# Out projection of a hybrid encoder layer: the residual rows of x read by plain loads and added by VectorE in place of accumulating DMAs

## The chip, the core and the metric

One core of a Trainium2 chip runs the whole layer as a single program. The metric is the device time of one execution in microseconds (us); the number compared is the median over runs. TensorE (PE) does the matmuls, ScalarE (ACT) and VectorE (DVE) empty its PSUM banks and do the elementwise work, GpSimd (POOL) does small scalar chains and issues the accumulating DMAs, and SyncE (SP) issues all other DMAs from one queue, in order.

## The reference, cut to what matters

The input `x` has 2048 rows (tokens) of 1024 floats. The layer mixes tokens, projects the mixed rows `y` with `w_out`, normalises the result and adds the input rows:

```python
y = jnp.concatenate([ya, yh.astype(ya.dtype)], axis=-1) @ w_out[l]
h = h + rms_norm(y, g_mix_post[l])          # h is x here
u = rms_norm(h, g_x_pre[l])
m = rms_norm(mem, g_mem[l])
y = cross_attention(u, m, wq_x[l], wk_x[l], wv_x[l], wo_x[l])
h = h + rms_norm(y, g_x_post[l])
```

The change concerns the second of these lines alone: `x` is added to the normalised projection. A SwiGLU feed-forward follows, with a residual of its own.

## The kernel before

The kernel works in fp32 and makes each product of two matrices from three products of rounded halves. The second half of the program is a list of **jobs** (`jobs`): the out projection, the cross-attention scores, the values, the feed-forward. A job is a list of blocks. A block of the out projection is 256 tokens (two row tiles of 128 tokens, `n` and `n + 1`) by all 1024 columns; the job has eight. By a Strassen scheme a block takes seven products instead of eight, so seven **steps**, each of 4 x 3 = 12 matmuls of 512 columns. The first two blocks and the last two run as pairs, their steps alternating; the four between run one by one.

`phases` walks through the steps. After the matmuls of a step it does the following, in this order: it notes the newest ACT and DVE instructions (`mark`), advances each open **after-generator** by one `yield`, splits a weight operand that has been loaded, and starts at most one load of half a weight operand for a coming step (`half`). The after-generator of a block is opened at the block's last step, so its work runs in the steps of the blocks behind it. `behind` ties the ACT and DVE instructions of its block to follow those that `mark` noted.

For the out projection, `mixed_block` gives a block its functions. `out` empties a PSUM bank into a row tile `y[i]` (lines 1377 and 1379) and takes its mean square on ACT (line 1355). `after`, the subject of the change, does in its successive steps: (1) the two inverse roots on POOL (1366 to 1370), the scaling of row tile 0 on DVE (1403), the accumulating DMA that adds 128 rows of x into it (`add`, line 1384, issued by POOL), and its store to `h1_d` (line 78, SP); (2) the same for row tile 1; (3) nothing; (4) and (5) the mean squares of the two sums on ACT; (6) their inverse roots on POOL; (7) and (8) the transposition of each row tile on PE (line 1270), copied back over the row tile by ACT (1271) and stored to `h1t_d`, from where the scores read it. `h1_d` and `h1t_d` are DRAM buffers; the profile cuts their names, so that a store into `h1_d` reads `h_d<-row`.

Row tiles, 128 x 1024 floats or 512 KB, come from a pool of nine (`row_tile`). The pool serves `y` of the blocks, every half operand that `half` loads for the next job (`row<-qk_d`, `row<-qk_s`), and one operand of `combined`, which prepares sums of weights beside the blocks (its add is line 929). The program's order on each engine is chosen at build time by a scheduler that gives a tile its buffer once an earlier holder has let it go; the instruction that first writes the tile then waits for that holder. On SP all that stands behind such a wait, or behind a store that waits for its data, waits too.

Of the kernel before, what the change touches and what calls it, by code (L numbers as in the profile page):

```python
# [15 lines left out]
ALU = mybir.AluOpType  # L16
# [32 lines left out]
class Layer:  # L49
# [1336 lines left out]
    def mixed_block(self, n):  # L1386
        nc = self.nc
        y, ss = {}, []

        def out(i, j, a, b):  # L1390
            if not y:
                ss.append(self.small("q_s", 4))
                if not n:
                    self.g_mix_post = self.gain(self.I["g_mix_post"])
            if i not in y:
                y[i] = self.row_tile()
            self.squared(y[i][:, j * 512:(j + 1) * 512], a, b, ss[0][:, 2 * i + j:2 * i + j + 1])

        def after():
            r = self.rstds(ss[0])  # L1400
            s2 = self.small("q_s", 4)
            for i in range(2):
                nc.vector.scalar_tensor_tensor(y[i], y[i], r[:, i:i + 1], self.g_mix_post, ALU.mult, ALU.mult)
                self.add(y[i], self.I["x"], n + i)
                self.store(self.h1_d[(n + i) * P:(n + i + 1) * P, :], y[i])
                yield
            yield
            for i in range(2):
                self.mean_squares(y[i], i, s2)
                yield  # L1410
            r = self.rstds(s2)
            nc.gpsimd.tensor_scalar(self.r_x[:, n:n + 2], r, 1.0, None, ALU.mult)
            yield
            for i in range(2):
                self.store(self.h1t_d[n + i], self.transposed(y[i], y[i]))
                yield

        return self.tokens(self.y_d, n), out, after, None

    def score_block(self, n):  # L1420
# [231 lines left out]
```

## Time and profile before

| | |
|---|---|
| time, median of 3 runs | 2605.68 us (2604.11 to 2606.04) |
| the profiled execution | 2605.43 us |
| its span in the profile | 2603.6 us |
| PE busy | 2526.8 us, 97% of the span |
| DVE, ACT, POOL busy | 1744.2, 1262.3, 473.4 us |
| DMA moved | 497.88 MB, mean 191 GB/s |
| matmuls of the out projection | about 802 to 985 us of the span |
| their accumulating DMAs of x | 16, issued from 846.9 to 992.1 us |

The profile is one execution, in us from the start of its span. "Busy" of PE counts time in which any matmul runs. A line such as `PE pss L1270 <- DMA row<-in_x_dram: 4.6, 2, 2.5` says that PE, before instructions of line 1270 that write a `pss` bank, stood idle for 4.6 us in all, twice, at most 2.5 us, until a DMA from x into a row tile had landed. In the view of windows each row has a stretch, its length, the busy us of each engine with the number of instructions in brackets, the granted clock of PE as a share of full speed, the mean busy share of the 16 DMA engines, and what they moved. Queue q0 carries the DMAs that POOL issues, q1 those of SP. In the chain of waits a row has the start, the length, and what took that time.

### The profile page before, as it was taken

How to read it: one execution, taken by the hardware profiler on the slowest of the kernel's cores; microseconds unless marked ns; L12 is line 12 of the kernel's file. 1: busy time of each engine (PE TensorE's matmuls, PEld its weight loads, DVE VectorE, ACT ScalarE, POOL GpSimd, SP SyncE). 2: the span in 40 equal slices, each digit the busy share in tenths (PEclk: the TensorE clock that was granted, in tenths of full speed). 3: DMA queues.
4: the chain of work that ended last, by engine and by line, in shares of the span. 5: the costliest groups of instructions: out<-in, count | busy, mean ns of one | idle time of the engine just before them, and what ended most of it. 6: DMA issues, size and time to landing. Idle time of an engine off the chain costs nothing.

```text
span 2603.6 us, 34511 instructions
## 1 busy us (share of the span) xinstructions
PE 2526.8 (97%) x12160; PEld 2112.8 (81%) x12160; DVE 1744.2 (67%) x2773; ACT 1262.3 (48%) x2641; POOL 473.4 (18%) x651
## 2 busy tenths in 40 slices
PE   7989999999998999999989999999999999999998
PEld 6878788878897777888878888888888888888786
DVE  7675578887555568786885655576666656664756
ACT  5463366655554556565573333354333335443443
POOL 4240343320321324223320000000000000000022
PEclk9999999999999999999999999999999999999999
DMA  5434655484876998756994532353556434576798
GB/s 186 142 121 166 208 157 173 131 265 158 265 253 219 281 318 265 228 193 173 306 282 145 164 128 73 105 187 114 168 181 230 148 107 168 175 225 176 229 226 210
DMA packets 286350, 497.88 MB, mean 191 GB/s; under 512 B 20576, under 2 KB 143456, under 8 KB 286176
## 3 DMA queue, kind: packets, MB, share of 16 engines
q1 hardware_dynamic: 275520, 456.87, 52.4%
q0 software_dynamic: 10656, 38.80, 8.0%
q8 instruction: 96, 1.57, 0.2%
q14 instruction: 78, 0.64, 0.1%
HBM read 328.87 MB, written 166.72 MB: 190 GB/s over the span
## 4 chain that ended last, share of the span: by engine, by line
PE 80%; DMA 8%; DVE 4%; issue 3%; POOL 2%; ACT 2%; SPq 0%; DVEq 0%; POOLq 0%; ACTq 0%
PE psm L1018 22%; PE psm L1020 22%; PE psm L1019 22%; PE psg L161 2%; PE psg L163 2%; PE psg L162 2%; DMA row<-in_x_dram 1%; PE pss L1270 1%; DMA row<-h_d 1%; ACT junk L1355 1%; DMA x<-in_w_out_dram 1%; DVE S L885 1%; DMA h_d<-row 1%; DMA pair<-in_x_dram 1%; DMA kk<-z_d 1%
## 5 line engine op out<-in xcount | busy, mean ns | idle before, releaser
L1018 PE MATMUL psm<-T,S 128*128 128x512 f32 x2664 | 1034.9, 392 | 24.6 <-ACT S L882 13.5
L1019 PE MATMUL psm<-T,S 128*128 128x512 f32 x2664 | 1041.1, 391 | 0.0
L1020 PE MATMUL psm<-T,S 128*128 128x512 f32 x2664 | 1036.1, 391 | 3.8 <-DVE S L885 3.8
L1018 PEld LDWEIGHTS psm<-T,S 128*128 128x128 f32 x2664 | 502.2, 189 | 132.7 <-ACT S L882 15.3
L1020 PEld LDWEIGHTS psm<-T,S 128*128 128x128 f32 x2664 | 501.9, 188 | 111.0 <-DVE S L885 6.9
L1019 PEld LDWEIGHTS psm<-T,S 128*128 128x128 f32 x2664 | 502.3, 189 | 103.0
L882 ACT ACTIVATE S<-sum 128x512 fp32r<-128x512 f32 (+1 forms) x338 | 208.1, 619 | 341.4 <-PE psm L1020 333.1
L885 DVE TENSOR_TENSOR S<-sraw,S 128x512 fp32r<-128x512 f32 (+1 forms) x311 | 214.2, 696 | 223.4 <-ACT S L882 213.4
L885 DVE TENSOR_TENSOR S<-sum,S 128x512 fp32r<-128x512 f32 (+1 forms) x404 | 276.8, 689 | 81.6 <-ACT S L882 63.7
L1033 ACT ACTIVATE part<-psm 128x512 f32<-128x512 f32 x297 | 175.1, 592 | 178.0 <-PE psm L1020 172.8
L882 ACT ACTIVATE S<-sraw 128x512 fp32r<-128x512 f32 (+1 forms) x272 | 166.8, 617 | 156.0 <-PE psm L1020 143.0
L1384 POOL DMA_DIRECT2D row<-y_d x28 | 25.0, 892 | 1132.5 <-DMA sraw<-hid_d 964.5
L1355 ACT ACTIVATE junk<-row 128x512 f32<-128x512 f32 x160 | 99.7, 625 | 118.2 <-DVE row L1377 34.9
L885 DVE TENSOR_TENSOR T<-row,T 128x1024 fp32r<-128x1024 f32 x104 | 123.1, 1191 | 30.5 <-ACT T L882 30.2
L161 PE MATMUL psg<-u,whi 128*128 128x512 f32 x352 | 141.1, 401 | 1.6 <-POOL whi L145 1.6
L163 PE MATMUL psg<-u,wlo 128*128 128x512 f32 x352 | 139.5, 396 | 0.9 <-DVE wlo L146 0.9
L162 PE MATMUL psg<-u,whi 128*128 128x512 f32 x352 | 139.6, 396 | 0.0
L882 ACT ACTIVATE T<-row 128x1024 fp32r<-128x1024 f32 x104 | 105.7, 1027 | 20.7 <-DMA row<-in_w_down_dram 10.3
L884 POOL TENSOR_SCALAR S<-sum 128x512 fp32r<-128x512 f32 x66 | 50.5, 765 | 238.7 <-PE psm L1020 148.3
L1536 DVE TENSOR_TENSOR part<-psm,part 128x512 f32<-128x512 f32 x66 | 45.4, 688 | 65.3 <-PE psm L1020 65.2
L146 DVE TENSOR_TENSOR wlo<-raw,whi 128x1024 fp32r<-128x1024 f32 x54 | 68.7, 1271 | 29.1 <-ACT whi L143 22.4
L1527 DVE TENSOR_TENSOR row<-psm,part 128x512 f32<-128x512 f32 x66 | 45.4, 689 | 57.6 <-PE psm L1020 57.5
(329 smaller groups left out, 3651.3 us busy)
## 6 DMA issues: line engine op xcount, KB each, us to landing
sraw<-in_w_gate_dram SPq DMA_DIRECT2D x44, 512.0 KB, 4.9
sraw<-in_w_up_dram SPq DMA_DIRECT2D x44, 512.0 KB, 4.8
hid_d<-row SPq DMA_DIRECT2D x44, 512.0 KB, 2.7
h_d<-row SPq DMA_DIRECT2D x32, 512.0 KB, 6.9
y_d<-row SPq DMA_DIRECT2D x32, 512.0 KB, 3.8
sraw<-hid_d SPq DMA_DIRECT2D x32, 512.0 KB, 5.2
row<-h_d POOLq DMA_DIRECT2D x30, 512.0 KB, 7.5
row<-y_d POOLq DMA_DIRECT2D x28, 512.0 KB, 7.3
```

What stands on the lines that cost most here:

```text
L146: nc.vector.tensor_tensor(lo, raw, f32(hi), ALU.subtract)
L161: nc.tensor.matmul(ps, ah, bh, start=(i == 0), stop=False)
L162: nc.tensor.matmul(ps, ah, bl, start=False, stop=False)
L163: nc.tensor.matmul(ps, al, bh, start=False, stop=(i == n - 1))
L882: self.nc.scalar.activation(hi, raw, AF.Copy)
L884: self.nc.gpsimd.tensor_scalar(hi, raw, 1.0, 1.0, ALU.mult, ALU.mult)
L885: self.nc.vector.tensor_tensor(lo, raw, f32(hi), ALU.subtract)
L1018: nc.tensor.matmul(ps, s[:, 0, k, :], t[:, 0, k, :], start=st, stop=False, **kw)
L1019: nc.tensor.matmul(ps, s[:, 0, k, :], t[:, 1, k, :], start=False, stop=False, **kw)
L1020: nc.tensor.matmul(ps, s[:, 1, k, :], t[:, 0, k, :], start=False, stop=sp, **kw)
L1033: nc.scalar.activation(t, ps, AF.Copy)
L1355: self.nc.scalar.activation(junk, a, AF.Square, scale=float(D) ** -0.5, accum_out=to)
```

## The change

In `after` of the out projection's blocks, two row tiles are taken at the first step and filled by plain loads of x from SP's queue (`rows_of`). The accumulating DMAs are gone; in their place DVE adds the loaded rows, in steps of their own. The sequence becomes: (1) two loads, the roots, the scaling of row tile 0; (2) the scaling of row tile 1; (3) add and store of row tile 0; (4) add and store of row tile 1; (5) and (6) the mean squares; (7) the roots; (8) and (9) the transpositions. The empty step is gone, and what follows it comes one step later.

```diff
         def after():
+            x = [self.rows_of(self.I["x"], n + i) for i in range(2)]
             r = self.rstds(ss[0])
             s2 = self.small("q_s", 4)
             for i in range(2):
                 nc.vector.scalar_tensor_tensor(y[i], y[i], r[:, i:i + 1], self.g_mix_post, ALU.mult, ALU.mult)
-                self.add(y[i], self.I["x"], n + i)
+                yield
+            for i in range(2):
+                with self.behind():
+                    nc.vector.tensor_tensor(y[i], y[i], x[i], ALU.add)
                 self.store(self.h1_d[(n + i) * P:(n + i + 1) * P, :], y[i])
                 yield
-            yield
             for i in range(2):
                 self.mean_squares(y[i], i, s2)
                 yield
```

## The prediction

> **What bounds the kernel now.** I read the page first, then the view of windows around the 16 accumulating DMAs.
>
> ```profile
> PE 2526.8 (97%) x12160; PEld 2112.8 (81%) x12160; DVE 1744.2 (67%) x2773; ACT 1262.3 (48%) x2641; POOL 473.4 (18%) x651
> ```
>
> ```profile
> 846.00:860.00 14.00, 14.00 (x68) 11.65 (x67) 10.58 (x13) 5.79 (x14) 6.76 (x7) 1.00 0.82 182
> 860.00:945.00 85.00, 77.21 (x365) 63.19 (x364) 46.68 (x61) 45.85 (x113) 27.32 (x49) 0.98 0.95 302
> 945.00:985.00 40.00, 39.91 (x184) 32.56 (x183) 32.81 (x40) 28.29 (x55) 10.79 (x16) 1.00 1.03 353
> 985.00:1020.00 35.00, 31.66 (x154) 25.72 (x153) 27.90 (x36) 21.77 (x51) 18.50 (x23) 1.00 0.92 270
> 1020.00:1180.00 160.00, 160.00 (x771) 133.35 (x770) 130.22 (x238) 94.83 (x221) 39.16 (x53) 1.00 0.61 204
> ```
>
> PE bounds the program: 97% busy. What a change outside PE can win is PE's idle time. From 846 to 1020 us that is 174 - (14.00 + 77.21 + 39.91 + 31.66) = 11.2 us, and the DMA engines are 82% to 103% busy there. From 1020 to 1180, with the DMA engines at 61%, PE never idles. So the stage with the adds is the one disturbed, and the transfers are what is tight in it. Next, who kept PE waiting in that stretch:
>
> ```profile
> PE pss L1270 <- DMA row<-in_x_dram: 4.6, 2, 2.5
> PE psm L1018 <- DVE row L1377: 2.7, 1, 2.7
> PE pss L1270 <- ACT row L1271: 2.5, 2, 2.1
> PE psm L1020 <- DVE S L885: 1.3, 1, 1.3
> ```
>
> These make 11.1 us, all of the idle time. The chain of waits tells what stood behind each:
>
> ```profile
> 878.23 8.85 DMA row<-in_x_dram
> 887.09 6.46 DMA h_d<-row
> ...
> 899.77 12.85 DMA extra<-qk_d
> ...
> 923.85 10.20 DMA row<-in_x_dram
> 934.18 1.83 PE pss L1270 x8
> 936.01 0.43 PE psm L1018
> ...
> 938.24 0.23 PE psm L1018
> ...
> 995.10 9.72 DMA g<-vo_d
> ```
>
> Two stalls (4.6 us) are PE itself waiting for an accumulating DMA before it can transpose the row tile. The second has a tail: PE comes back at half speed, 0.43 us a matmul against 0.23, for five matmuls (1.0 us), and eight transpositions take 1.83 us where 0.88 is the full-speed length in the same chain:
>
> ```profile
> 967.01 0.88 PE pss L1270 x8
> ```
>
> That is 0.95 more, so a tail of about 1.9 us. The 2.5 us behind ACT are a step further on: ACT copies the transposed tile back over the row tile, must wait until the store of h1 has read it, and that store waits for the accumulating DMA. The 2.7 us hang on a weight load that took 12.85 us in the crowded DMA engines while DVE, in order, stood at line 929; the 1.3 us on another such load (9.72 us). Two more views show how far the accumulating DMA holds others, first ACT's waits, then SP's:
>
> ```profile
> ACT junk L1355 <- DMA row<-in_x_dram: 29.2, 8, 8.1
> ```
>
> ```profile
> SPq L78 <- DMA row<-in_x_dram: 54.3, 13, 9.5
> ```
>
> **The change part by part.** *Removed: 16 accumulating DMAs.* The view of DMA from 820 to 1010 us gives the price of a transfer of either kind.
>
> ```profile
> q1 hardware_dynamic: 16337, 43.18, 62.9%
> q0 software_dynamic: 2304, 8.39, 23.5%
> ...
> row<-in_x_dram POOLq DMA_DIRECT2D x16, 512.0 KB, 9.7
> h_d<-row SPq DMA_DIRECT2D x16, 512.0 KB, 7.3
> row<-qk_d SPq DMA_DIRECT2D x14, 512.0 KB, 6.8
> ...
> extra<-qk_d SPq DMA_DIRECT2D x3, 512.0 KB, 8.6
> ```
>
> q0 is the 16 adds: 23.5% of 190 us is 44.7 us of all engines, 2.79 us each. q1 moved 43.18 MB in 62.9%, 119.5 us, so 1.45 us for each 0.524 MB. A plain load in place of an add saves 1.34 us, 21 us for 16: the load on the engines over these 190 us falls from 86% to 75%. POOL loses 16 issues, which cost it a cheap row:
>
> ```profile
> L1384 POOL DMA_DIRECT2D row<-in_x_dram x16: 857/892/1176, 846.9 to 992.1; - x16
> ```
>
> These 0.9 us each I count as nothing, POOL being busy 18% of the span. The transposition and ACT's squares no longer wait for a transfer issued after the scaling: I take the 4.6 us and the 1.9 us as won. h1's store now waits for a DVE add, and SP is not held for 54.3 us; the 2.5 us go too (bounds 0 and 2.5: the store still takes its 7.3 us, but it starts two steps, 5.6 us, behind the scaling, where today it starts when 9.7 us of transfer have landed). Of the 2.7 us I take half, since it was the crowd that made 12.85 us out of a median of 8.6; of the 1.3 us nothing, as DVE is at its fullest there. Together 4.6 + 1.9 + 2.5 + 1.3 = 10.3 us, between 4.6 (the direct waits alone) and 13.0 (everything).
>
> *Added: 16 DVE adds.* Line 929 is the same operation on the same shape, beside it the scaling that stays:
>
> ```profile
> L929 DVE TENSOR_TENSOR extra<-extra,row x6: 1211/1218/1225, 847.3 to 937.8; 128x1024 f32<-128x1024 f32 x6
> ```
>
> 16 x 1.22 = 19.5 us of DVE. From 846 to 1020 DVE is busy 117.97 of 174 us, 68%, and would be 79%. The row 1020 to 1180 shows DVE at 130.22 of 160, 81%, with PE not idle at all, so over the mean the cover is there: bound 0. It is thin from 945 to 1020: 60.71 of 75 us, and the adds of three blocks, 7.3 us, make it 91%. If all of those stood in PE's way the cost would be 7.3; I take 3, nearer to the row without a stall.
>
> *Moved: stores, squares, transpositions one step later.* A step is 12 x 0.23 = 2.8 us. The readers of h1t come whole blocks later (84 x 0.23 = 19 us each), which hides it; without that cover it would cost 2.8 us once.
>
> *Added: 16 loads through SP and the pool of nine row tiles.* SP already waits for row tiles, as the loads held until a weight split or a store of h1t lets one go show:
>
> ```profile
> SPq L75 <- DVE T L885: 5.2, 6, 2.6
> ...
> SPq L75 <- DMA h1t_d<-row: 4.6, 3, 2.2
> ```
>
> ```profile
> 946.41 5.09 SPq L75 DMA_DIRECT2D row<-qk_d  x3
> ...
> 959.66 5.34 SPq L75 DMA_DIRECT2D row<-qk_s  x3
> ```
>
> From 946 on nine are not enough: three loads take 5 us to issue. Each x tile is held for a landing (6.8) and about two steps (5.6), some 12 us, so the last three blocks ask for 6 x 12 = 72 tile-us more, 8 us of the whole pool. Behind a load that waits stand the token loads `sraw` and the stores. The weight operands of the scores are split from 958 on and first used at 985, a margin of 27 us which would hide 8. Bounds 0 and 8, taken 1.
>
> Two DVE inputs in SBUF are the subject of a rule that speaks against the change. Rows of POOL and DVE:
>
> ```profile
> 849.68 1.45 POOL L884 TENSOR_SCALAR S<-sraw 128x512 fp32r<-128x512 f32 x1
> ...
> 863.78 0.62 POOL L884 TENSOR_SCALAR S<-sum 128x512 fp32r<-128x512 f32 x1
> ```
>
> ```profile
> 849.12 3.08 DVE L1403 SCALAR_TENSOR_TENSOR row<-row,q_r,g 128x1024 f32<-128x1024 f32 x2
> ```
>
> POOL's split takes 0.62 us alone and 1.45 beside a DVE scaling with two SBUF inputs. The Trainium skill ("SBUF — State Buffer", section "SBUF: two separate sides") says the same in general: a DVE operation with two SBUF inputs and a GpSimd operation that reads SBUF exclude one another for a whole instruction. The trace agrees, 0.8 us longer in that pair. By it 21 splits of POOL, each with a chance of 19.5/174 to meet an add, lose 21 x 0.11 x 1.2 = 2.8 us on POOL, and if PE felt all of it the sum below would be 2601.9 instead of 2599.1.
>
> **The sum.** 2605.43 (the profiled execution; span 2603.6 and 1.8 around it; 0.25 below the median of the runs) - 10.3 + 3 + 1 = 2599.1 us.
>
> **The rivals.**
>
> *A: the stall moves.* The waits for the transfer go, but the last three blocks and the start of the scores pay for row tiles and for a DVE at 91%. For it: the slot waits and the window 945 to 985, where PE has no idle time to win and DVE is at 82%. Against it: the margin of 27 us. Price: 7.3 for DVE and 1 for slots in place of 4: 2605.43 - 10.3 + 8.3 = 2603.4, no change that can be told.
>
> *B: the wait goes from POOL and ACT to DVE.* The add stands in DVE's in-order queue, and everything PE lives on (the splits, the emptied banks) stands behind it. It decides from the point at which x lands later than the two steps, 5.6 us, that lie between its issue and its add. For it, line 929, which is such an add behind a load:
>
> ```profile
> DVE extra L929 <- DMA extra<-qk_d: 6.8, 1, 6.8
> ...
> DVE extra L929 <- DMA g<-vo_d: 3.5, 1, 3.5
> DVE extra L929 <- DMA row<-qk_d: 2.7, 1, 2.7
> ```
>
> Three of nine waited, 13.0 us, and PE lost 2.7 + 1.3 of it, 0.31 us for each us; x lands in 9.7 us today, plain row tiles in 6.8, and a full pool delays the issue itself. If x keeps 9.7 us and a full pool adds 5 to the issue, each of eight blocks holds DVE for 9.1 us: 73 us x 0.31 = 22.6 us. 2605.43 - 10.3 + 22.6 = 2617.7; without the 5 us it is 4.1 x 8 x 0.31 = 10.2, as much as the gain. Against it: the load needs no data from the block, so the scheduler may issue it as soon as a tile is free, before the step in which it is written; 6.8 us of landing is then covered.
>
> Should the loads be issued only with the scaling or behind it, because no tile is free, then x is not loaded beside the norm and the change does not do what it says: that is B with its 5 us.
>
> **How the numbers follow.** 0.2%, 5.2 us, is about what can be told from no change here. The forecast has 0.46; its own range is 2592.4 (all 13.0 us won, nothing paid) to 2602. A has 0.24, B 0.30. Faster by over 5.2 us: the forecast but for its upper edge, 0.44. Within: A and that edge, 0.26. Slower: B, 0.30, from 2611 to 2620. The range 2592.4 to 2614 holds all of the forecast and of A, and a third of B.
>
> **What would show each step.** Right: no wait of PE, ACT or SP for a DMA from x; idle time of PE from 846 to 1020 of 5 us or less; no half-speed matmuls around 936; q0 gone from the stage and the DMA share there near 0.8; DVE near 79% with no long wait at the new add. A shows as idle time of PE between 985 and 1020, loads on SP waiting for row tiles; B as DVE waiting several times for a DMA from x at the new add, and PE behind it for line 885 or 882. Wrong would be an end above 2602 with those waits gone, which would mean that the stalls were not theirs.

## The result and the profile after

| | before | changed |
|---|---|---|
| median, 13 runs each, taken side by side | 2608.14 us (2603.32 to 2611.53) | 2613.03 us (2609.32 to 2620.17) |
| ratio to the kernel before | | 1.0019, 95% interval 1.0012 to 1.0026 |
| once more, 11 runs against 32 | 2610.21 us | 2614.0 us, ratio 1.0014 (1.0005 to 1.0023) |

The change makes the kernel some 4 to 5 us slower, where 6 us of gain were forecast. Two profiles of each kernel were taken. Up to the out projection both programs have the same instructions in the same order, yet its first matmul came between 800.0 and 810.0 us in the fourteen profiles of this study, by chance: the first profile of the changed kernel (810.0) must not be read window by window against that of before (801.9). Its second, which starts at 801.4, can be. The same windows as in the prediction, of the second profile of the changed kernel:

```profile
846.00:860.00 14.00, 10.23 (x44) 8.15 (x43) 12.79 (x15) 4.18 (x10) 1.73 (x2) 0.89 0.52 181
860.00:945.00 85.00, 85.00 (x412) 71.01 (x411) 60.03 (x74) 49.29 (x119) 22.70 (x44) 1.00 0.92 315
945.00:985.00 40.00, 40.00 (x186) 33.30 (x185) 35.98 (x42) 30.05 (x55) 14.62 (x16) 1.00 0.92 314
985.00:1020.00 35.00, 29.41 (x129) 22.89 (x129) 25.86 (x35) 17.34 (x42) 14.09 (x15) 0.90 0.71 238
1020.00:1180.00 160.00, 159.88 (x769) 133.12 (x768) 131.67 (x238) 96.50 (x225) 38.24 (x53) 1.00 0.61 204
```

From 860 to 985 PE no longer idles at all (85.00 of 85.00 us, where it had 77.21). But 3.8 us of idle time stand before 860 and 5.6 behind 985, where PE also runs at 0.89 and 0.90 of its clock. Who kept PE waiting, same profile, from 803 to 1180 us:

```profile
PE pss L1270 <- ACT row L1271: 4.3, 3, 2.1
PE pss L1270 <- DVE row L1408: 3.5, 1, 3.5
PE psm L1020 <- DVE S L885: 0.9, 1, 0.9
PE psm L1018 <- ACT S L882: 0.6, 2, 0.3
```

No wait for a DMA from x is left. New is a wait for line 1408, the add on DVE. What that line did, from its own view:

```profile
L1408 DVE TENSOR_TENSOR row<-row,row x16: 1206/1212/1630, 849.4 to 1005.6; 128x1024 f32<-128x1024 f32 x16
...
its engine sat idle before it (us, times) until:
who waited for it (us, times):
  ACT junk L1355: 4.1, 1
  PEld pss L1270: 3.9, 1
  PE pss L1270: 3.5, 1
```

Nothing stands under "its engine sat idle before it": DVE never waited for a row of x. To see by stage what came and went, I took the starts of PE's matmuls of lines 1018 to 1020 from the traces: a block is 84 of them, so each stretch below holds the same work in every kernel, whatever came ahead. In brackets the idle time of PE; columns are stretches in us. "Blocks 0 to 3" begins with the first matmul of the out projection, and the first pair's work behind its matmuls falls into it; "scores 0, 1" is the first pair of the scores, into which the last pair's work falls.

```
                    blocks 0-3   blocks 4,5   blocks 6,7   scores 0,1   scores 2,3   scores 4-7  values
before              87.2 (2.6)   49.0 (5.2)   41.5 (0.1)   45.8 (3.3)   43.2 (0.0)   82.1        172.5
before, again       87.8 (3.5)   47.9 (4.1)   41.8 (0.0)   45.7 (3.3)   43.1 (0.0)   82.1        174.1
changed             89.5 (3.8)   41.7 (0.0)   40.9 (0.0)   51.6 (5.4)   45.2 (1.4)   81.6        174.5
changed, again      88.4 (3.8)   41.7 (0.0)   40.9 (0.0)   51.4 (5.6)   44.2 (0.1)   81.6        174.2
e1_first            89.5 (3.8)   41.7 (0.0)   40.9 (0.0)   49.6 (5.8)   44.3 (0.9)   82.1        175.3
e2_last             86.4 (2.9)   47.2 (3.4)   42.9 (1.4)   50.6 (6.1)   43.9 (0.0)   81.6        173.6
e3_shift            89.4 (3.2)   43.6 (1.5)   42.8 (1.5)   47.6 (3.9)   43.9 (0.4)   82.1        173.6
e4_pool             88.1 (3.3)   43.6 (1.5)   44.9 (1.8)   53.5 (6.9)   45.0 (1.6)   82.1        174.9
e5_late6            89.4 (3.8)   41.7 (0.0)   40.9 (0.0)   43.7 (2.8)   48.8 (3.2)   83.4        174.0
e6_noload           86.7 (3.0)   47.0 (4.8)   41.7 (0.4)   50.2 (5.2)   44.4 (0.3)   81.6        173.7
e7_singles          84.5 (1.2)   41.3 (0.0)   41.4 (0.0)   49.3 (5.0)   44.2 (0.7)   82.1        172.6
e8_stag4            84.6 (1.3)   41.7 (0.0)   40.9 (0.0)   45.0 (2.3)   44.4 (0.0)   81.6        173.9
e9_bstag4           82.6 (0.3)   48.7 (4.8)   43.0 (0.7)   46.1 (3.6)   49.6 (3.4)   81.6        173.6
e10_stag4_last      89.3 (3.8)   41.7 (0.0)   40.9 (0.0)   48.0 (4.8)   44.4 (0.0)   81.6        171.9
```

Means of the two profiles of either kernel: the middle blocks gain 6.75 + 0.75 = 7.5 us, the larger part of the 10.3 that the prediction expected of the waits. The first pair's stretch loses 1.45, the first two score stretches 5.75 + 1.55 = 7.3; the rest of the scores gives 0.5. So the stage is level (+0.75 us) in spite of the gain, and the rest of the 4 to 5 us stands behind it: the values 1.05 and the last 300 us of the program 1.4, each within the 1.6 that before's own two profiles differ by there, and the first eight blocks of the feed-forward 1.55 (163.1 and 163.0 before, 164.5 and 164.7 after). The 820 us between agree in all profiles.

What happens at the first pair shows in the chain of waits, second profile of the changed kernel (start, length, what):

```profile
847.87 0.15 DVE row L1404
...
849.43 1.21 DVE row L1408
...
851.17 0.68 DVE S L885
851.85 1.14 DVE row L1408
852.98 1.13 DVE extra L929
854.12 0.60 DVE S L885
854.72 1.13 DVE row L1408
855.86 0.60 DVE row L1377
856.46 1.14 DVE row L1408
857.60 0.04 issue
857.64 1.97 PE pss L1270 x8
859.61 0.43 PE psm L1018
860.04 0.43 PE psm L1019
```

Two blocks end one step apart, so four scalings and four adds come to DVE in one bunch, among the splits PE lives on. PE, whose order was fixed at build time, stands 3.50 us for the bunch's last add before it may transpose; then come eight transpositions in 1.97 us instead of 0.88, and two matmuls of 0.43 us. At the last pair the bunch meets the splits of the scores' weights. DVE there, second profile of the changed kernel, ten microseconds a row:

```profile
980.00:990.00 10.00, 10.00 (x48) 8.27 (x47) 10.00 (x10) 3.93 (x9) 5.06 (x4) 1.00 0.78 248
990.00:1000.00 10.00, 8.54 (x41) 6.59 (x40) 10.00 (x16) 2.29 (x5) 5.01 (x2) 1.00 0.60 216
1000.00:1010.00 10.00, 6.21 (x20) 4.32 (x19) 6.75 (x9) 7.61 (x21) 5.49 (x7) 0.69 0.53 201
```

DVE is busy for 20 us without a gap; in the last row PE gets through 20 matmuls at 0.69 of its clock.

PE waits there three times for line 1271, ACT's copy into a row tile (4.3 us in the view of waits). Before the first wait, 0.5 us, ACT itself waits for a store of h1. Before the longest, 2.1 us, the chain passes through POOL (second profile of the changed kernel):

```profile
995.29 4.46 POOL x_mr L1439
1000.00 0.28 issue
1000.28 0.77 ACT row L1441 x3
1001.05 0.95 ACT T L882
1002.00 0.48 ACT row L1271
```

Line 1439 is a small step of the scores, 128x2 numbers. Here it takes 4.75 us (4.74 in the first profile); the first two of the kernel before (line 1436 there) took 0.27 us each. All the while DVE ran without a gap on SBUF tiles, two adds of line 1408 and four instructions of lines 885 and 987, and POOL was done 0.25 us after DVE had gone on to line 1433, which reads PSUM. So DVE seems to have held POOL up; no run isolates it. ACT, in order, stood 3.6 us for POOL, and its next copy for PE came late.

### The profile page after: what moved, and what is told of

Its sections match the earlier page's. It is cut to its first block, busy times and chain, and to the rows that moved or that the text cites. A ratio compares the mean times of both kernels' runs of the same rounds, so it can differ in the third digit from the quotient of the medians.

```text
span 2618.5 us, 34517 instructions
## 1 busy us (share of the span) xinstructions
PE 2535.1 (97%) x12160; PEld 2119.3 (81%) x12160; DVE 1762.2 (67%) x2789; ACT 1262.7 (48%) x2641; POOL 466.0 (18%) x635
## 5 line engine op out<-in xcount | busy, mean ns | idle before, releaser
L882 ACT ACTIVATE S<-sraw 128x512 fp32r<-128x512 f32 (+1 forms) x272 | 167.0, 617 | 164.8 <-PE psm L1020 151.4
```

The source lines that it names most:

```text
L882: self.nc.scalar.activation(hi, raw, AF.Copy)
```

## The experiments

Theory S: the waits for the accumulating DMA are gone, but the adds of the paired blocks fall in bunches on a DVE that is full there. At first S named the last pair alone. Rivals: R, the row tiles the loads of x take; M, the moved steps; N, chance between profiles; and, once a cure was tried, G, the cure alone.

**e0_again**, the changed kernel without an edit.

> The changed kernel once more, for a second profile and a second comparison. Theory S (the stall moves: the waits for the accumulating DMA are gone, and the start of the scores pays because the last pair's adds of x fall where DVE is full): out projection about 172 us against 177.7 before, scores 175 to 179 against 171.1, total 3 to 6 us above the kernel before. Theory N (the two profiles differ by chance alone): the stage lengths swing by as much again between the two profiles of the same kernel, 5 us or more.

Ratio 1.0014 (1.0005 to 1.0023). The stretches agree with the first profile within 1.1 us; N is out for the stage: its gains and losses are much larger. The scores' total, 177.2, lies in the range S gave.

**e1_first and e2_last**, the change in a part of the blocks:

```diff
+            if n < NT - 4:
                 x = [self.rows_of(self.I["x"], n + i) for i in range(2)]
...
+            else:
...
```

(in e2_last the condition is `n >= NT - 4`; behind `else` stand the steps of the kernel before)

> Six blocks get the change, the last pair keeps its accumulating DMAs. Theory S: the out projection keeps most of its 5 us gain and the scores return to about 171 us, so 2 to 6 us below the kernel before, 7 or more below the changed kernel. Rival R (row tiles: 16 more tenants of the nine delay loads all along the stage): the six blocks carry 12 of the 16 tiles, so most of the loss stays, 2 to 5 us above the kernel before.

> Only the last pair gets the change, six blocks keep their accumulating DMAs. Theory S: no gain in the out projection and the loss in the scores, 5 to 10 us above the kernel before. Rival R: 4 of 16 tiles, at most 2 us above.

e1_first: 1.0000 (0.9989 to 1.0012). e2_last: 1.0022 (1.0012 to 1.0033), 6 us, though it makes only 4 of the 16 adds. So the last pair alone can make a loss of this size, and the number of row tiles does not set it: R had 2 us at most. But e1_first missed what S gave it: the last pair behind new neighbours costs 49.6 us though its adds are the old ones (its waits: 2.3 us for the DMA from x, 3.5 for ACT), and the first pair still bunches (89.5 us). S, which had 2 to 6 us of gain here, was too narrow: the first pair costs too, and the start of the scores loses without any DVE add in the last pair.

**e3_shift**, the moved steps with the old DMA:

```diff
-            x = [self.rows_of(self.I["x"], n + i) for i in range(2)]
...
-                with self.behind():
-                    nc.vector.tensor_tensor(y[i], y[i], x[i], ALU.add)
+                self.add(y[i], self.I["x"], n + i)
```

> The accumulating DMAs stay and only the steps move: both scalings first, then an accumulating DMA and a store in each of the next two steps, everything behind them one step later. Theory S: the adds are what costs, so 0 to 3 us above the kernel before (the accumulated rows come later by two steps). Rival M (the moved steps cost, whatever does the add): 4 to 8 us above, with the scores near 178 us.

1.0007 (0.9998 to 1.0015). Scores 0 and 1 take 47.6 us, 1.85 above before: the moved steps are a third of the 5.75 lost there. M falls. They also win: blocks 4 and 5 take 43.6, perhaps because an accumulating DMA two steps behind the scaling holds others less; no run isolates that.

**e4_pool**, POOL adds:

```diff
-                    nc.vector.tensor_tensor(y[i], y[i], x[i], ALU.add)
+                    nc.gpsimd.tensor_tensor(y[i], y[i], x[i], ALU.add)
```

> As the changed kernel, but POOL adds x instead of DVE: same loads, same row tiles, same steps. Theory S (DVE full at the start of the scores): the stalls there shrink and the time falls by 2 to 5 us below the changed kernel, unless POOL holds DVE up in its place, which would show as DVE instructions lengthened beside the adds. Rival R (row tiles): the same 3 to 6 us above the kernel before as the changed kernel.

1.0035 (1.0024 to 1.0045), the slowest of all. The condition that S named came true. POOL's adds, and DVE's groups from 846 to 1020 us in this kernel (last, busy us and mean ns of one):

```profile
L1408 POOL TENSOR_TENSOR row<-row,row x16: 2402/3111/3976, 846.5 to 998.7; 128x1024 f32<-128x1024 f32 x16
```

```profile
L885 DVE TENSOR_TENSOR S<-sraw,S 128x512 fp32r<-128x512 f32 x22 | 25.6, 1177 | 5.0 <-POOL S L884 4.2 <-ACT S L882 0.8
L1404 DVE SCALAR_TENSOR_TENSOR row<-row,q_r,g 128x1024 f32<-128x1024 f32 x15 | 25.4, 1731 | 1.2 <-POOL q_r L1370 1.2
...
L929 DVE TENSOR_TENSOR extra<-extra,row 128x1024 f32<-128x1024 f32 x6 | 12.3, 2046 | 3.9 <-DMA row<-qk_d 2.9 <-DMA extra<-qk_d 1.0
```

The same in the second profile of the changed kernel:

```profile
L1404 DVE SCALAR_TENSOR_TENSOR row<-row,q_r,g 128x1024 f32<-128x1024 f32 x14 | 18.1, 1331 | 2.0 <-POOL q_r L1370 2.0
...
L885 DVE TENSOR_TENSOR S<-sraw,S 128x512 fp32r<-128x512 f32 x24 | 16.3, 685 | 8.9 <-ACT S L882 5.4 <-POOL S L884 3.6
...
L929 DVE TENSOR_TENSOR extra<-extra,row 128x1024 f32<-128x1024 f32 x6 | 7.3, 1220 | 5.9 <-DMA row<-qk_d 3.8 <-DMA extra<-qk_d 1.1 <-DMA qk_s<-extra 0.9
```

A split goes from 685 to 1177 ns, line 929 from 1220 to 2046. So the run does not separate S from R: it took 19.8 us of adds off DVE and lengthened what DVE kept.

**e5_late6**, the last pair's work six steps later:

```diff
+            for _ in range(6 if n >= NT - 4 else 0):
+                yield
             x = [self.rows_of(self.I["x"], n + i) for i in range(2)]
```

> As the changed kernel, but the last pair starts its work behind the matmuls six steps later, so that loads, scalings, adds, squares and transpositions of these four row tiles fall behind the splits of the scores' weights. Theory S (a crowd on DVE and ACT there): the gain of the out projection stays, about 7 us in blocks 4 and 5, and the start of the scores loses 2 us or less instead of 5.7, so 2 to 6 us below the kernel before. Rival R: four tiles of y held six steps longer, so loads and p tiles come later and the time is 3 or more above the changed kernel.

1.0004 (0.9995 to 1.0013). Scores 0 and 1 take 43.7, 2 less than before, but scores 2 and 3 take 48.8 and the rest 83.4: the three stretches sum to 175.9, against 177.8 changed and 171.0 before. S had 2 to 6 us of gain and missed; R, with 3 or more above the changed kernel, missed too. The loss moved with the pair's work. So the weights' splits alone do not make it; that the pair's own bunch does is what the next runs try.

**e6_noload**, e2_last without loads:

```diff
-                x = [self.rows_of(self.I["x"], n + i) for i in range(2)]
+                x = [self.g_mix_post, self.g_mix_post]
```

> As e2_last (the change in the last pair alone), but without its four loads of x: DVE adds the gain tile, which is there anyway, so the output lacks x in these 512 rows. It keeps the four DVE adds and the moved steps and takes no row tiles and no transfers. Theory S: as e2_last, 4 to 8 us above the kernel before. Rival R: no loss, within 2 us of the kernel before.

1.0009 (1.0000 to 1.0018), between the two. By stage: scores 0 and 1 take 50.2 us without the loads and their tiles, 50.6 with them. The loss at that place needs neither tiles nor transfers; DVE's adds and the moved steps are enough for it. Whether the loads add something elsewhere the two totals leave open, since their intervals overlap.

**e7_singles**, the change in the four single blocks alone (`if 4 <= n < NT - 4`):

> The change only in the four blocks that run one by one; both pairs keep their accumulating DMAs. Theory S: blocks 4 and 5 keep 41.7 us against 48 before, the 3.5 us stall of the first pair's adds is gone, and the start of the scores has no adds to crowd it, so 45.7 to 49.6 us there (e1_first had 49.6 with the old last pair): 2 to 6 us below the kernel before. If the old last pair behind new blocks costs as in e1_first, no difference.

0.9993 (0.9983 to 1.0003), no difference, where S had 2 to 6 us of gain. The stall of the first pair is gone (84.5), blocks 4 and 5 gain (41.3), and the old last pair gives much of it back (49.3, of which PE waits 3.3 us for the DMA from x).

**e8_stag4**, the whole change, with the second block of either pair four steps later:

```diff
+            for _ in range(4 if n in (2, NT - 2) else 0):
+                yield
             x = [self.rows_of(self.I["x"], n + i) for i in range(2)]
```

> The whole change, but in each of the two pairs the second block starts its work behind the matmuls four steps after the first, so that two scalings and two adds on DVE come in a row instead of four. Theory S: the 3.5 us stall of the first pair goes, the start of the scores is 46 to 49 us instead of 51.5, and the time is 1 to 5 us below the kernel before. If it is the amount of work on DVE there and not its bunching, 51 us stay and the time is as the changed kernel's.

2599.96 us, ratio 0.9969 (0.9959 to 0.9979): faster than both kernels by more than S forecast: 8.8 us below the kernel before in the medians, where S had 1 to 5. The first pair's stretch falls to 84.6, scores 0 and 1 to 45.0, the middle blocks keep theirs. PE's waits from 803 to 1180 us are down to one row:

```profile
PE psm L1018 <- ACT part L1033: 3.5, 2, 2.3
```

The windows of e8_stag4 up to 1020 us, to be held against those of the changed kernel above:

```profile
846.00:860.00 14.00, 14.00 (x68) 11.58 (x66) 12.86 (x17) 5.40 (x13) 2.87 (x3) 1.00 0.48 144
860.00:945.00 85.00, 83.73 (x406) 69.71 (x405) 64.42 (x78) 47.86 (x120) 26.31 (x44) 1.00 0.96 343
945.00:985.00 40.00, 40.00 (x186) 33.30 (x185) 36.11 (x41) 30.11 (x56) 14.50 (x16) 1.00 0.89 315
985.00:1020.00 35.00, 32.75 (x154) 26.96 (x153) 32.51 (x52) 23.27 (x62) 13.12 (x20) 0.95 0.80 283
```

The instructions are the same. DVE is busy for 145.9 of 174 us, 84%, more than the 134.7 (77%) of the changed kernel in the same window, and PE idles 3.5 us instead of 9.4. It is the bunch, not the sum of DVE's work: in the first row DVE is as busy as in the changed kernel (12.86 against 12.79 us), yet PE never waits. At the scores a full DVE is not what tells the two apart: counted from the first matmul of the scores, the 20 us shown above for the changed kernel are 975.9 to 995.9 here, and DVE is busy for 20.00 of them too. What differs is the order: the first two POOL steps of line 1439 (line 1441 here) take 1.20 and 2.29 us, not 4.75. And the stagger spreads all that the second block does behind its matmuls, ACT's, POOL's and SP's part too. So DVE's part is shown at the first pair, where PE stood for line 1408 itself; at the scores it is argued. DVE waits here twice for a load of x, 3.4 us in all, as rival B feared, and PE loses nothing by it.

**e9_bstag4**, the control: the kernel before, with that stagger and nothing else.

> The kernel before with nothing but the stagger: its accumulating DMAs stay, and the second block of each pair starts its work four steps later. Theory S (the DVE adds bring 7 us in blocks 4 and 5, the bunch takes it back, the stagger mends the bunch): blocks 4 and 5 stay at 48 us, so the time is within 3 us of the kernel before. Rival G (the stagger alone makes the gain, whatever adds x): 5 to 9 us below the kernel before.

1.0015 (1.0004 to 1.0025), 3.4 us above in the medians, just outside the 3 us that S gave. Blocks 4 and 5 stay at 48.7, the first pair gains 4.9 by the stagger alone, and scores 2 and 3 lose 6.5. G falls: the gain of the whole needs both, the adds on DVE for the single blocks and the stagger for the pairs.

**e10_stag4_last**, the stagger in the last pair alone.

> The whole change with the stagger in the last pair alone. Theory S: the first pair's stall of 3.5 us and its half clock come back (88.9 us for blocks 0 to 3 against 84.6), the start of the scores stays at 45: 3 to 6 us above e8_stag4, 2 to 6 below the kernel before. If the first pair does not matter, as e8_stag4.

0.9993 (0.9983 to 1.0003). The first pair is back at 89.3 with its 3.5 us; scores 0 and 1 take 48.0, 3.5 less than the changed kernel, 3.0 more than e8_stag4 (PE idle 4.8 us there against 2.3). The time lies 1 to 2 us below the kernel before, where S had 2 to 6. So either pair counts, but S had 45 for the start of the scores: how the first pair reaches so far is not shown. Each edit makes the scheduler order anew what follows, and some us between two variants may come from that.

**b0_again**, the kernel before against itself.

> The kernel before against itself: what two profiles of one program differ by. Ratio 1.000 within 0.001. Its first profile has no half clock at the start of the scores and one of 3.4 us in the values and the out projection together; theory S and rival R both expect the same stalls at the same places (the two transpositions behind the DMA from x, the one at line 1377, the one at the start of the scores, some 11 us in all), with half-clock stretches coming or not by chance where a stall is over 2 us.

1.0007 (0.9997 to 1.0018). The stalls came back in the same places, and the stretches agree within 1.1 us up to the values, which differ by 1.6. The totals of all profiles differ by more, through the 800 us ahead of the stage.

## Why the prediction was wrong

*The removed waits: right.* No engine waits for a DMA from x, and the middle blocks gain 7.5 us. With the bunches spread (e8_stag4) the whole out projection takes 167.2 us instead of 177.65, 10.4 us less, where 10.3 were reckoned; the match is partly luck, since 2.1 of the 10.3 were a stall at the start of the scores. So the prediction's own sign of being wrong, an end above 2602 with those waits gone, came true, but not what it was to mean: the stalls were those of the waits. Two sizes were off. The DMA engines were to fall from 86% to 75% of 190 us; second profile of the changed kernel, 820 to 1010 us:

```profile
q1 hardware_dynamic: 18825, 51.78, 79.1%
...
row<-in_x_dram SPq DMA_DIRECT2D x16, 512.0 KB, 6.9
h_d<-row SPq DMA_DIRECT2D x16, 512.0 KB, 5.0
```

They fell to 79%, and a store of h1 lands in 5.0 us (median) instead of 7.3. And SP is not free: its stores, which waited 54.3 us for the DMAs from x, now wait for the adds. SP's waits from 803 to 1020 us, second profile:

```profile
SPq L78 <- DVE row L1408: 33.9, 12, 15.1
```

*The DVE adds: the step that failed.* The duration was right (1.21 us each). The prediction said "over the mean the cover is there: bound 0", counted the adds of three blocks behind 945 us, and took 3 of 7.3 us. It left out that `before` runs its first and last two blocks as pairs, whose work behind the matmuls starts one step apart. The mean over 174 us says nothing of a bunch of eight DVE instructions of 1.2 to 1.4 us in 15 us. The stretches put the cost of the bunches, changed against staggered, at 88.95 - 84.6 = 4.35 us for the first pair and 177.8 - 171.0 = 6.8 for the scores, 11.2 in place of 3. With that term the prediction's sum is 2605.43 - 10.3 + 11.2 + 1 = 2607.3, 1.9 above its start; the measured difference is 4 to 5.

*The tail of half speed* was reckoned for the stall that went, not for those that might come. Scores 0 and 1 have 2.2 us more idle time than before but take 5.75 more; the granted clock is at half for 6.8 us in both profiles of the changed kernel there, and not at all in before's.

*The row tiles: taken 1, measured 0.4* at the start of the scores and 1.2 in blocks 6 and 7 (e6_noload against e2_last), one profile each, where two profiles of one kernel differ by up to 1.1. The margin they had was smaller than reckoned: by the count of matmuls the scores begin at 979.6 us in the first profile of the kernel before, not at 985, so 21.6 us behind the first weight split and not 27.

*POOL beside DVE:* the prediction named it, priced it at 2.8 us on POOL, and left it out of its sum. The 4.75 us of line 1439 at the start of the scores look like it; the price of 1.2 us for each meeting had no place for one POOL instruction behind six of DVE in a row.

*Rival A was what came*, at its place, the start of the scores, and, as far as the rows tell, by its cause, a DVE at its limit, but priced at no change, since it counted the end of the stage alone and no half speed. *Rival B fell*: DVE never waited at line 1408, as the loads were issued ahead of the step that uses them (the first at 839.8 us in the first profile, the first add at 857.7) and landed in 6.9 us. Its price was also misread: the view of DVE's waits has a fourth wait at line 929, 2.4 us, so the rate is 4.0 of 15.4 us, 0.26, and not 0.31.

*Open:* the 2 to 3 us that the sum still lacks, of which 1.55 show in the first eight blocks of the feed-forward. The order of its instructions differs from kernel to kernel, and other variants take 161.3 to 164.8 us there; no run isolates it.

## What to carry to other kernels

Work taken from a DMA and given to an engine that paces PE is paid where it comes in a bunch ahead of what the other engines wait for, not at the mean share: look in the trace for such places (paired blocks, the seam between two stages), and reckon the cost there. When a change gains in the regular part and loses at the ends, spread the ends before giving it up: four empty steps for two blocks turned a loss of 0.19% into a gain of 0.31%. And run the cure on the old kernel too, to see that it is not the cure alone.

## What the runs showed of the hardware

A POOL add of two 128x1024 row tiles takes 3.11 us (median) beside a working DVE, where DVE's takes 1.21, and some of DVE's instructions with two SBUF inputs grow by up to 72% around it (685 to 1177 ns, 1220 to 2046 ns). The Trainium skill ("SBUF — State Buffer", section "SBUF: two separate sides") says that a DVE operation with two SBUF inputs and a GpSimd operation that reads SBUF lock one another out; the numbers of e4_pool agree.

The same stall does not always cost the same: 3.5 us before the first pair's transpositions was followed by 6.8 us at half clock in one profile of the changed kernel and by 3.4 in the other, and before's 2.1 and 1.3 us at the start of the scores by none. Stalls of 2.2 and 2.5 us could be enough for it: in the second profile of the kernel before 3.4 us at half clock followed on each, while in its first profile 2.7 us were followed by none.
